# First-half attention units over natural keys in one softmax, and class-ordered copies of the second-half queries

## The chip, the core and the metric

One core of a Trainium2 chip runs the whole kernel. Its engines work side by side, each with its own queue: TensorE (PE in the profile; PEld is its loading of stationary operands), VectorE (DVE), ScalarE (ACT), GpSimd (POOL), and SyncE (SP), which issues nearly all DMAs. The metric is the device time of one execution in microseconds (us). The kernel before took 1133.38 us in the median of three runs (1132.27 to 1135.93).

## The reference

One decoder layer: sequence 1024, width 1024, float32. The input is normalised and projected once; a quarter of the width goes through causal mean pools, three quarters through 12 attention heads of 64; both results share one output projection; then follows a gated feed-forward block. Each head is attended three times, with keys at distances up to 128 (every key), up to 512 (every 4th) and up to 2048 (every 16th), and the three results are merged by their softmax denominators:

```python
DILATED_CONFIGS = ((128, 1), (512, 4), (2048, 16))
for window, dilation in DILATED_CONFIGS:
    o, lse = dilated_branch(q, k, v, window, dilation)   # softmax of s over valid keys; o = e/den @ v
w = softmax(stack(lses), axis=0)
o = sum(w[..., None] * stack(outs), axis=0)
```

Merging by denominators is the same as one softmax over the union of the three key sets in which a key that belongs to two or three of them counts twice or three times.

## The kernel before

All products run on TensorE with float32 data split in a high and a low part: a projection step is three 512-column matmuls. Every matmul is recorded at L276 (`mm`), every transpose at L279 (`turned_to`).

Attention is cut into 12 **units**: six head pairs, each with a first half (queries 0 to 511, `h = 0`) and a second half (queries 512 to 1023, `h = 1`). A unit treats two heads and has four kinds of steps:

- *Scores* (`scores`, L705 on). Each head has a natural side (`side 0`, mask `mA`, the last 128 keys) and a class side (`side 1`, mask `mB`, positions that agree modulo 4). For each of four blocks of 128 queries two matmuls, for the high and the low query part (`qh`, `ql`), write one row block to a PSUM bank with tag `s`, of which there are two. On the class side the stationary operand is `slice(j, 512, 4)`, every fourth query. Where `sg` is 0, `pull()` puts one or more projection matmuls (the *filler*) ahead of each such score matmul. DVE takes the bank with mask and minimum (L750), ACT takes the exponential with its sum (L753).
- *Join* (`merge`, `join`, L758 on). The two sides have their own minima and sums; eleven small DVE instructions, an exponential and two tiny matmuls (`ps_s<-ex,ls`) bring them to common weights `wv`.
- *Weighing* (`weigh`, L801 on). 16 scalings of `pp` by `wv`, most on POOL (L816), some on DVE (L814) or ACT (L812).
- *Values* (`values`, L844 on). `turn` transposes up to four 128 x 128 blocks to a bank `t` (two banks) and splits them to `ptr` (ACT L861, DVE L862); `product` multiplies them by `v`, high and low part. The groups are listed in `GROUPS` (L836).

Keys are stored by class (`k`, position modulo 4 outermost); natural key blocks are read with a strided view. The value rows are in DRAM (`vd`); `v_load` (L672 on) loads a natural (`v0`) and a class-ordered (`v1`) copy for each half.

Order: `put(steps, lo, hi)` places steps on a time axis whose unit is one attention unit, from numbers in `PRM` (L30 to L260); `emit` sorts all steps by these places. A clock with estimated latencies (`await_`) may pull filler steps ahead of a step that would wait. TensorE keeps exactly the written order (`keep_in_program_order`); on the other engines a scheduler places the instructions by priority (`rank`, table `hk`), and each engine then works through its queue in order. Each PE wait in the attention part therefore stops the whole PE stream behind it.

Of the kernel before, what the change touches and what calls it, by code (L numbers as in the profile page):

```python
# [8 lines left out]
F32 = mybir.dt.float32  # L9
# [34 lines left out]
 'n0': 0.12632,
 'n1': 0.36647,
 'h0': {'s0': 0.02145,
        's1': 0.42346,
        'm': 0.62035,
        'w0': 0.78144,
        'w1': 1.2041,  # L50
        't0': 0.85648,
        't1': 1.83344,
        'v0': 1.2506,
        'v1': 2.02168},
 'h1': {'s0': 0.0,
        's1': 0.55,
        'm': 0.63061,
        'w0': 0.77607,
        'w1': 1.33988,
        't0': 0.97415,  # L60
        't1': 1.84958,
        'v0': 1.09414,
        'v1': 1.95434,
        'u0': 0.15852,
        'u1': 0.10633,
        'u2': 0.23141,
        'u3': 0.53154},
# [12 lines left out]
 'pe': 1,  # L80
 'cut': {7: (1, 6, 17)},
# [1846 lines left out]
```

## Time and profile before

| | us |
|---|---|
| median of three runs | 1133.38 |
| the profiled execution's own time | 1133.22 |
| its span in the profile | 1131.4 |
| PE busy | 1115.9 |
| DVE busy | 806.1 |
| ACT busy | 559.9 |
| POOL busy | 549.0 |

Attention runs from about 55 to 400 us of the span, the output projection and the norms until about 490, and the feed-forward block to the end. A matmul's busy time in the profile is longer than its share of the stream, since matmuls overlap; the pitch, from one start to the next, is what the stream pays. Rows of the timeline give the start and the length of a run of like instructions, so the next row's start gives the pitch.

### The profile page before, as it was taken

The page shows a single profiled execution, that of the slowest core. Times are in us where ns is not written, and L with a number is a line of the kernel's source. Part 1 is how long each engine was busy: PE and PEld are TensorE (multiplying, and loading weights), DVE is VectorE, ACT ScalarE, POOL GpSimd, SP SyncE. Part 2 cuts the span into 40 slices and gives each one's busy share as a digit, 9 for nine tenths or more (in the row PEclk, how much of TensorE's full clock was granted, in tenths as well). Part 3 has the DMA queues.
Part 4 walks back from the last instruction along what each step waited for, and adds up shares of the span by engine and source line. Part 5 has one row for each costly group of instructions (what it writes and reads, how often), then busy time and mean ns, then how long its engine had stood idle before and what let it go on. Part 6 is the DMA issues. An engine that isn't in the chain of part 4 may idle for free.

```text
span 1131.4 us, 16902 instructions
## 1 busy us (share of the span) xinstructions
PE 1115.9 (99%) x5922; PEld 958.3 (85%) x5922; DVE 806.1 (71%) x1516; ACT 559.9 (49%) x1068; POOL 549.0 (49%) x481
## 2 busy tenths in 40 slices
PE   9999999999999999999999999999999999999997
PEld 7888999999898888888888888888888888888896
DVE  7967888887998675989777777665676462343684
ACT  8466667666677563966422222332222534343441
POOL 0122646253466222010267767775577896666521
PEclk9999999999999999999999999999999999999999
DMA  8215242415146555672566666434444896556442
GB/s 283 93 70 187 80 146 75 149 57 168 57 130 219 193 191 218 262 280 109 200 235 242 235 233 233 168 143 163 169 168 176 287 348 220 188 195 202 132 149 75
DMA packets 91156, 201.59 MB, mean 178 GB/s; under 512 B 9280, under 2 KB 25152, under 8 KB 89664
## 3 DMA queue, kind: packets, MB, share of 16 engines
q1 hardware_dynamic: 90096, 199.74, 50.5%
q8 instruction: 46, 0.75, 0.3%
q10 hardware_dynamic: 976, 0.79, 0.2%
q14 instruction: 38, 0.31, 0.1%
HBM read 143.61 MB, written 56.89 MB: 177 GB/s over the span
## 4 chain that ended last, share of the span: by engine, by line
PE 90%; DVE 5%; DMA 2%; POOL 1%; ACT 1%; issue 1%; ACTq 0%; SPq 0%; POOLq 0%
PE ps_pj L276 27%; PE ps_s L276 26%; PE ps_o L276 24%; PE ps_t L276 10%; PE ps_t L279 2%; DMA mixd<-mix 1%; POOL pp L816 1%; DVE pp L750 1%; DVE ptr L862 1%; DMA m<-mixd 1%; DVE rsw L512 0%; ACT pp L753 0%; DVE ql L544 0%; DMA wraw<-in_w_in_dram 0%; DVE rco L513 0%
## 5 line engine op out<-in xcount | busy, mean ns | idle before, releaser
L276 PE MATMUL ps_o<-tT,fw 128*128 128x512 f32 x648 | 150.5, 389 | 0.0
L276 PEld LDWEIGHTS ps_o<-tT,fw 128*128 128x128 f32 x648 | 121.5, 188 | 25.4 <-DVE p L1551 0.2
L276 PE MATMUL ps_pj<-x,whl 128*128 128x512 f32 x480 | 138.1, 407 | 0.3 <-DVE whl L324 0.3
L816 POOL TENSOR_SCALAR pp<-pp,wv 128x256 f32<-128x256 f32 (+1 forms) x135 | 67.4, 518 | 111.8 <-DVE wv L796 111.8
L1368 POOL TENSOR_TENSOR fw<-rw,fw 128x512 fp32r<-128x512 f32 x72 | 99.8, 1409 | 31.1 <-ACT fw L1366 31.1
L753 ACT ACTIVATE pp<-pp,sx 128x128 f32<-128x128 f32 (+1 forms) x192 | 89.3, 467 | 32.2 <-DVE sx L750 31.5
L276 PEld LDWEIGHTS ps_pj<-x,whl 128*128 128x128 f32 x480 | 85.0, 189 | 11.1 <-DVE whl L324 0.7
L1663 POOL TENSOR_TENSOR op<-rw,op 128x512 fp32r<-128x512 f32 x38 | 62.2, 1636 | 31.2 <-ACT op L1662 30.6
L350 POOL TENSOR_TENSOR nrr<-nrr,half 128x4 f32<-128x4 f32 (+1 forms) x7 | 7.1, 1013 | 144.3 <-ACT eps L349 102.3
L324 POOL TENSOR_TENSOR whl<-wraw,whl 128x512 fp32r<-128x512 f32 x42 | 54.7, 1323 | 45.7 <-ACT whl L320 43.5
L276 PE MATMUL ps_s<-b,fw 128*128 128x512 f32 x312 | 72.5, 389 | 0.0
L276 PEld LDWEIGHTS ps_s<-b,fw 128*128 128x128 f32 x312 | 58.6, 188 | 12.2
L276 PE MATMUL ps_pj<-whl,x 128*128 128x256 f32 (+1 forms) x432 | 68.4, 300 | 0.0
L1366 ACT ACTIVATE fw<-rw 128x1024 fp32r<-128x1024 f32 x45 | 47.5, 1061 | 41.4 <-PE ps_o L276 16.3
L1368 POOL TENSOR_TENSOR whl<-rw,whl 128x512 fp32r<-128x512 f32 x30 | 47.0, 1587 | 42.4 <-ACT whl L1366 20.8
L1662 ACT ACTIVATE op<-rw 128x1024 fp32r<-128x1024 f32 x38 | 40.0, 1059 | 55.3 <-PE ps_t L276 35.8
L862 DVE TENSOR_TENSOR ptr<-ps_t,ptr 128x512 fp32r<-128x512 f32 (+1 forms) x84 | 55.3, 665 | 11.5 <-ACT ptr L861 10.6
L861 ACT ACTIVATE ptr<-ps_t 128x512 fp32r<-128x512 f32 (+1 forms) x84 | 47.3, 577 | 26.7 <-PE ps_t L279 23.4
L276 PEld LDWEIGHTS ps_pj<-whl,x 128*128 128x128 f32 x432 | 58.2, 191 | 1.7
L1664 DVE TENSOR_TENSOR op<-rw,op 128x512 fp32r<-128x512 f32 x33 | 28.5, 864 | 40.2 <-ACT op L1662 36.1
L276 PE MATMUL ps_s<-k,qh 128*128 128x128 f32 (+1 forms) x192 | 54.3, 294 | 1.9 <-DVE sx L750 1.5
L276 PE MATMUL ps_o<-ptr,v 128*128 128x128 f32 (+1 forms) x472 | 55.5, 255 | 0.2 <-DVE ptr L862 0.2
(328 smaller groups left out, 2856.1 us busy)
## 6 DMA issues: line engine op xcount, KB each, us to landing
rw<-bd SPq DMA_DIRECT2D x77, 256.0 KB, 4.0
rw<-in_w_gate_dram SPq DMA_DIRECT2D x28, 512.0 KB, 4.7
rw<-in_w_up_dram SPq DMA_DIRECT2D x28, 512.0 KB, 5.6
v<-vd SPq DMA_DIRECT2D x22, 512.0 KB, 4.8
rw<-wsd SPq DMA_DIRECT2D x44, 256.0 KB, 3.9
bd<-p SPq DMA_DIRECT2D x39, 256.0 KB, 2.0
rw<-in_w_down_dram SPq DMA_DIRECT2D x33, 256.0 KB, 4.1
wraw<-in_w_out_dram SPq DMA_DIRECT2D x15, 512.0 KB, 4.5
```

Source lines behind the costliest of these rows:

```text
L276: return tc.keep_in_program_order(nc.tensor.matmul(*a, **k))
L279: return tc.keep_in_program_order(nc.tensor.transpose(dst, src, by))
L324: pin(eng.tensor_tensor(dst[:, 1, at:at + w], src[:, at:at + w], dst[:, 0, at:at + w].bitcast(F32), ALU.subtract))
L753: nc.scalar.activation(pt[:, j, lo:], pt[:, j, lo:], AF.Exp, bias=sx[:, 0, side, j, hd, 0:1], scale=-1.0, accum_out=sx[:, 0, side, j, hd, ...
L816: nc.gpsimd.tensor_scalar(pv, pv, un.wv[:, side, j, hd:hd + 1], 1.0, op0=ALU.mult, op1=ALU.mult)
L861: nc.scalar.activation(ptr[:, 0, :w], t[:, :w], AF.Copy)
L862: nc.vector.tensor_tensor(ptr[:, 1, :w], t[:, :w], ptr[:, 0, :w].bitcast(F32), ALU.subtract)
L1366: nc.scalar.activation(dst[:, :, 0], src, AF.Copy)
L1368: low[0] = eng.tensor_tensor(dst[:, i, 1], src[:, i], dst[:, i, 0].bitcast(F32), ALU.subtract)
L1662: nc.scalar.activation(w[:, :, 0], raw, AF.Copy)
L1663: nc.gpsimd.tensor_tensor(w[:, 0, 1], raw[:, 0], w[:, 0, 0].bitcast(F32), ALU.subtract)
L1664: (nc.gpsimd if p == "P1" else nc.vector).tensor_tensor(w[:, 1, 1], raw[:, 1], w[:, 1, 0].bitcast(F32), ALU.subtract)
```

## The change

1. **First-half units** (`dense`, new). The 512 queries see only keys 0 to 511, so each query block of 128 is scored once against all natural keys up to its own (128, 256, 384 or 512 columns). A new mask `mD` (128 x 512, one more load) adds the logarithm of how often a key counts. One softmax gives the weights: no join, no `ex` matmuls; `factor` takes one reciprocal per head. A bank holds one 512-wide row block, or 384 + 128, or 256 + 256. There are 8 scalings instead of 16 (`dense_step`), 10 transposes a head instead of 11, and 4 key blocks of value products, each for all later queries at once, from `v0` alone.
2. **Second-half units** (`q_classes`, new). The queries are copied to class order once per unit (`qc`): the high part by two copies on POOL, the low part by two on ACT (`qe`), 0.3 of a unit ahead of it (`qc: -0.3`). The class-side score matmuls read 128 adjacent queries from `qc`. The `pull()` ahead of each is gone, and `sg` with it. The join is split: its first two DVE instructions (`others`), then an `await_`, then the rest.
3. `v_load` loads `v0` of the first half alone at first, then the other three.
4. Most of the numbers in `PRM` are new: places of steps, priorities, which engine takes a scaling, a split or a rope addition.

Counted over the program, TensorE has 5640 matmuls and transposes written instead of 5856, that is 36 fewer a pair: 16 scores, 2 transposes, 16 value products, 2 `ex`. DVE has 144 mask-and-minimum instructions instead of 192, each with its read, 58 fewer two-operand ones and 15 fewer scalings. POOL has 88 scalings instead of 135, 12 copies and 6 more two-operand instructions.

Three places in the order of instructions. First TensorE in the first half of pair 1 (unit 2). `qh`, `ql_97` are the query parts, `k` the keys, `x_...,whl` is filler for the next pair's projections. Before, at one of its class-side groups:

```order
L276 MATMUL ps_pj<-x_121,whl 128x512
L276 MATMUL ps_s<-k,qh 128x128
L276 MATMUL ps_pj<-x_121,whl 128x512
L276 MATMUL ps_s<-k,ql_97 128x128
L276 MATMUL ps_pj<-x_121,whl 128x512
L276 MATMUL ps_s<-k,qh 128x128
L276 MATMUL ps_pj<-x_122,whl 128x512
L276 MATMUL ps_s<-k,ql_97 128x128
```

Now, the first three of the unit's five score steps:

```order
L287 MATMUL ps_s<-k,qh 128x512
L287 MATMUL ps_s<-k,ql_97 128x512
L287 MATMUL ps_pj<-x_118,whl 128x512 x3
L287 MATMUL ps_s<-k,qh 128x384
L287 MATMUL ps_s<-k,ql_97 128x384
L287 MATMUL ps_s<-k,qh 128x128
L287 MATMUL ps_s<-k,ql_97 128x128
L287 MATMUL ps_pj<-x_119,whl 128x512 x3
L287 MATMUL ps_pj<-x_120,whl 128x512 x3
L287 MATMUL ps_s<-k,qh 128x256
L287 MATMUL ps_s<-k,ql_97 128x256
```

The alternation of narrow scores and single filler matmuls is gone; fewer and wider scores stand in runs, with filler in threes between them.

Second, TensorE at the second half of pair 4 (unit 10), around the values of unit 9 (`ptr`). Before:

```order
L276 MATMUL ps_s<-k,qh 128x256
L276 MATMUL ps_s<-k,ql_97 128x256
L276 MATMUL ps_s<-k,qh 128x256
L276 MATMUL ps_s<-k,ql_97 128x256
L276 MATMUL ps_pj<-whl,x_120 128x256 x3
L276 MATMUL ps_pj<-whl,x_121 128x256 x3
L279 MATMUL ps_t<-pmt,pp 128x128 x4
L276 MATMUL ps_s<-k,qh 128x256
L276 MATMUL ps_s<-k,ql_97 128x256
L276 MATMUL ps_s<-k,qh 128x256
L276 MATMUL ps_s<-k,ql_97 128x256
```

Now:

```order
L290 MATMUL ps_t<-pmt,pp 128x128 x7
L287 MATMUL ps_pj<-whl,x_122 128x256 x3
L287 MATMUL ps_pj<-whl,x_123 128x256 x3
L287 MATMUL ps_s<-k,qh 128x256
L287 MATMUL ps_s<-k,ql_97 128x256
L287 MATMUL ps_s<-k,qh 128x256
L287 MATMUL ps_s<-k,ql_97 128x256
L287 MATMUL ps_s<-k,qc 128x256 x8
L287 MATMUL ps_o<-ptr,v_3837 128x4x4x32
L287 MATMUL ps_o<-ptr,v_3837 64x4x4x32
```

Before, other work stood between two groups of four score matmuls; now three groups, which need three banks of the two, stand in one run (one with `qh` and `ql`, two with `qc`).

Third, POOL around the query copies of pair 1 (`wd` are the new first-half weights, `whl<-wraw` the split of a projection weight). Before, from the scalings of that pair's first half on:

```order
L816 TENSOR_SCALAR pp<-pp,wv 128x128 x3
L816 TENSOR_SCALAR pp<-pp,wv 128x256
L816 TENSOR_SCALAR pp<-pp,wv 128x128 x4
L816 TENSOR_SCALAR pp<-pp,wv 128x256 x3
L324 TENSOR_TENSOR whl<-wraw,whl 128x512 x2
L514 TENSOR_TENSOR rsw<-rsw,sinr 128x512
L517 TENSOR_TENSOR rcl<-rco,rsw 128x128x4
```

Now:

```order
L905 TENSOR_SCALAR pp<-pp,wd 128x384
L905 TENSOR_SCALAR pp<-pp,wd 128x256
L652 COPY qc<-qh 128x512 x2
L335 TENSOR_TENSOR whl<-wraw,whl 128x512 x4
L529 TENSOR_TENSOR rcl<-rco,rsw 128x128x4
```

There are two scalings here where eleven were, the copies stand behind them, and behind the copies stand the weight splits for the filler.

The diff, cut to its core (of the table of numbers a few lines):

```diff
- 'we': (1, 1, 0, 0, 0, 0, 1, 0, 0, 1, 1, 1),
+ 'we': (1, 0, 1, 0, 0, 0, 0, 0, 0, 0, 1, 0),
...
+        'qc': -0.3},
...
- 'sg': (0, 0, 0, 0, 0, 1, 0, 0, 0, 0, 1, 1),
- 'tv': (0, 0, 0, 0, 0, 1, 0, 0, 1, 0, 0, 1),
+ 'tv': (0, 1, 0, 1, 0, 1, 0, 1, 1, 1, 0, 0),
+ 'dw': (0, 0, 0, 2, 1, 0, 0, 0),
...
+ 'qe': ((0, 2), (0, 2), (0, 2), (0, 2), (0, 2), (0, 2))}
...
+    mD = cload(maskD, [P, 512], "mD", qkp)
...
+    def q_classes(pr):
+        pr.qc = []
+        for n in range(2):
+            src = pr.q[1][n]
+            to = qkp.tile([P, 2, 512], F32R, name="qc", tag="qc%d" % n, bufs=1)
+            by, from_ = to.rearrange("p a (c r) -> p a c r", c=4), src.rearrange("p a (r c) -> p a c r", c=4)
+            eng = G["qe"][pr.p][n]
+            for a in range(2):
+                if eng == 2:
+                    nc.scalar.activation(by[:, a], from_[:, a], AF.Copy)
+                else:
+                    (nc.vector if eng else nc.gpsimd).tensor_copy(by[:, a], from_[:, a])
+            pr.qc.append(to)
...
-        return [lambda h=h: load(h) for h in range(2)]
+        return [lambda: load((0, 0)), lambda: load((1, 0), (1, 1), (0, 1))]
...
+    def dense(pr, un):
+        un.sx = small.tile([P, 2, 2, 4], F32, name="sd", tag="sd", bufs=2)
...
+            for hd, j in blocks:
+                w = (j + 1) * P
+                so[hd, j] = s[:, at:at + w]
+                at += w
+                for n in range(2):
+                    mm(so[hd, j], q[n][:, hd, j * P:(j + 1) * P], view(pr.k[:, hd], 0, [[P, 4], [1, 32 * (j + 1)]]),
+                       start=(n == 0), stop=(n == 1))
...
+                    nc.vector.tensor_tensor_reduce(
+                        by_rows, by_class(so[hd, j]), mD[:, 512 - (j + 1) * P:].rearrange("p (r c) -> p r c", c=4),
+                        op0=ALU.add, op1=ALU.min, scale=-0.125, scalar=3e38, accum_out=sx[:, 0, hd, j:j + 1])
+                    nc.scalar.activation(r, r, AF.Exp, bias=sx[:, 0, hd, j:j + 1], scale=-1.0,
+                                         accum_out=sx[:, 1, hd, j:j + 1])
...
+                nc.vector.reciprocal(un.wv[hd], un.sx[:, 1, hd])
...
+        return [lambda: step([(0, 3)]), lambda: step([(0, 2), (0, 0)]), lambda: last(0, (0, 1), (1, 1)),
+                lambda: step([(1, 3)]), lambda: last(1, (1, 2), (1, 0))]
...
-            q, kc = pr.q[h], pr.k
+            q, kc = pr.qc if side else pr.q[h], pr.k
...
-                qs = slice(j * P, (j + 1) * P) if side == 0 else slice(j, 512, 4)
+                qs = slice(j * P, (j + 1) * P)
...
-                    if side and not G["sg"][turn_of(pr, h)]:
-                        pull()
...
-    GROUPS = ([[(1, r, r, 1) for r in range(4)],
-               [(0, 0, 0, 1), (0, 0, 1, 0), (0, 1, 1, 1), (0, 1, 2, 0)],
-               [(0, 2, 2, 1), (0, 2, 3, 0), (0, 3, 3, 1)]],
+    GROUPS = ([[(0, j) for j in range(4)], [(1, j) for j in range(1, 4)], [(2, 2), (2, 3), (3, 3)]],
...
+            if h == 0:
+                for kb in sorted({kb for kb, j in g}):
+                    wd = (4 - kb) * P
+                    oo = view(o[hd], 32 * kb, ([[32, 4 - kb]] if kb < 3 else []) + NAT)
+                    v = pr.v[0, 0][:, kb, hd]
+                    mm(oo, v.rearrange("p a f -> p (a f)"), ptr[:, 0, n * P:n * P + wd],
+                       start=(kb == 0), stop=False, skip_group_check=True)
+                    mm(oo[0:64], v[:, 0], ptr[:, 1, n * P:n * P + wd], start=False, stop=(kb == 3), skip_group_check=True)
+                    n += 4 - kb
...
+        if h:
+            put([lambda pr=pr: q_classes(pr)], u + g["qc"], 0)
+            put([lambda a=(pr, h): merge(*a)], u + g["m"], 0)
```

More of the change, by code (lines that the diff above doesn't have):

```diff
@@ new lines @@
+        'u2': 0.41454,
+        'u3': 0.53154,
+        'qc': -0.3},
+ 'f0': 7e-05,
+ 'f1': -0.00185,
+ 'first': {'s0': 0.526,
+           's1': 0.68454,
+           'm': 0.84275,
+           'w0': 0.75,
+           'w1': 0.96155,
+           't0': 1.1,
+           'v0': 1.3,
+           'v1': 1.94598},
+ 'vt': ((1.09517, 1.10518),
+        (2.83002, 3.26626),
+        (4.77155, 5.38909),
+        (6.76078, 7.29364),
+        (8.75641, 10.31491),
+        (9.91793, 10.41054)),
+ 'pw': (-0.11144, -0.10043, -0.01308),
@@ L758, in merge @@
     def merge(pr, h):
-        with tc.high_priority(offset=rank("j", pr, h)):
-            join(pr, h)
-    def join(pr, h):
         need(("s", pr.p, h), 8)
@@ L766, in join, with others @@
         un = pr.un[h]
+        with tc.high_priority(offset=rank("j", pr, h)):
+            ex = others(un)
+        due["e",] = clock[0] + G["je"]
+        await_(("s", 0), ("e",))
+        with tc.high_priority(offset=rank("j", pr, h)):
+            join(un, ex)
+        for i in range(17):
+            due["w", pr.p, h, i] = clock[0] + G["lw"][0] + G["lw"][1] * i
+    def others(un):
+        ex = small.tile([P, 2, 4, 4, 4], F32, name="ex", tag="ex", bufs=1)
+        own = un.sx[:, 0].rearrange("p s j a b -> p s j (a b)")
+        for sd in range(2):
+            nc.vector.tensor_tensor(ex[:, sd], own[:, 1 - sd][:, None].to_broadcast([P, 4, 4, 4]),
+                                    qd[1 - sd][:, :, None, None].to_broadcast([P, 4, 4, 4]), ALU.mult)
+        return ex
+    def join(un, ex):
         sx = un.sx
-        ex = small.tile([P, 2, 4, 4, 4], F32, name="ex", tag="ex", bufs=1)
-        own = sx[:, 0].rearrange("p s j a b -> p s j (a b)")
         e = bank("s")
@@ L848, in values, with weighted @@
         turned, o = {}, {}
+        def weighted(hd, gi):
+            return "w", pr.p, h, (8 * hd + 8 - 4 * groups[gi][0][0] if h else 4 * hd + 4)
         def turn(hd, gi):
             g = groups[gi]
-            need(("w", pr.p, h, hd, g[0][0]), 4)
-            await_(("t", 0), ("w", pr.p, h, 8 * hd + 8 - 4 * g[0][0]))
+            if h:
+                need(("w", pr.p, h, hd, g[0][0]), 4)
+            else:
+                need(("w", pr.p, 0, hd), 4)
+            await_(("t", 0), weighted(hd, gi))
             t = bank("t")
-            for n, (side, kb, qs, part) in enumerate(g):
+            for n, (kb, j) in enumerate(g if h == 0 else ()):
+                turned_to(t[:, n * P:(n + 1) * P], un.row(hd, j)[:, kb * P:(kb + 1) * P], pmt)
+            for n, (side, kb, qs, part) in enumerate(g if h else ()):
                 turned_to(t[:, n * P:(n + 1) * P], un.pp[hd, side][:, qs, part * P:part * P + P],
@@ L911, in both @@
                 await_(*([("t", 0), ("t", 1)] if new else []),
-                       *(("w", pr.p, h, 8 * hd + 8 - 4 * groups[gi][0][0]) for hd, gi in new),
+                       *(weighted(*a) for a in new),
                        *(("ptr", pr.p, h, *a) for a in old), ("v", pr.p, h))
```

155 lines of the change are left out of this document (96 added, 59 removed), and 320 rows, old and new, of the table PRM.

## The prediction

> **What bounds the kernel now.** I read the page, then the busy time by stage, then PE's waits, then the stream itself.
>
> ```profile
> span 1131.4 us, 16902 instructions
> PE 1115.9 (99%) x5922; PEld 958.3 (85%) x5922; DVE 806.1 (71%) x1516; ACT 559.9 (49%) x1068; POOL 549.0 (49%) x481
> ...
> PE 90%; DVE 5%; DMA 2%; POOL 1%; ACT 1%; issue 1%; ACTq 0%; SPq 0%; POOLq 0%
> ```
>
> PE is busy for all but 15.5 us, and the chain that ended last is 90% PE. By stage (window, its length, then busy PE, PEld, DVE, ACT, POOL, clock, DMA share, GB/s):
>
> ```profile
> 0.00:55.00 55.00, 53.27 (x233) 43.23 (x234) 47.36 (x70) 34.40 (x50) 5.45 (x10) 1.00 0.56 192
> 55.00:400.00 345.00, 337.48 (x2261) 308.42 (x2260) 279.13 (x833) 232.25 (x628) 148.21 (x193) 1.00 0.38 127
> 400.00:900.00 500.00, 500.00 (x2306) 416.15 (x2305) 361.23 (x461) 198.85 (x283) 264.09 (x197) 1.00 0.56 205
> 900.00:1131.40 231.40, 225.20 (x1128) 190.50 (x1126) 118.38 (x154) 94.43 (x109) 131.24 (x82) 0.99 0.58 192
> ```
>
> The change works in the second row. PE idles 345 - 337.5 = 7.5 us there, in waits like these:
>
> ```profile
> PE ps_t L279 <- POOL pp L816: 2.0, 1, 2.0
> PE ps_o L276 <- DVE dhl L999: 1.6, 2, 0.9
> ...
> PE ps_s L276 <- DVE sx L750: 1.5, 3, 0.7
> PE ps_pj L276 <- DMA m<-mixd: 1.2, 1, 1.2
> ```
>
> So attention is bound by the length of the PE stream. Removed PE work shortens the kernel one for one as long as the other engines feed the rest; removed DVE or ACT work shortens nothing by itself, and at most 7.5 us of idle can go.
>
> **Prices of the PE stream.** These timeline rows (start, length, group, count) give the pitches; the next row's start is what counts.
>
> ```profile
> 117.75 0.22 PE L276 MATMUL ps_s<-k,qh 128*128 128x128 f32 x1
> 117.81 0.45 PE L276 MATMUL ps_pj<-x,whl 128*128 128x512 f32 x1
> 118.10 0.22 PE L276 MATMUL ps_s<-k,ql 128*128 128x128 f32 x1
> ...
> 128.60 0.23 PE L276 MATMUL ps_s<-k,qh 128*128 128x128 f32 x1
> ...
> 129.06 0.60 PE L279 MATMUL ps_t<-pmt,pp 128*128 128x128 f32 x4
> 129.42 0.71 PE L276 MATMUL ps_o<-ptr,v 128*128 128x256 f32 x4
> 129.97 0.28 PE L276 MATMUL ps_s<-k,qh 128*128 128x256 f32 x1
> ...
> 130.44 0.64 PE L276 MATMUL ps_pj<-whl,x 128*128 128x256 f32 x4
> ...
> 136.61 0.55 PE L276 MATMUL ps_s<-ex,ls 128*128 128x64 f32 x4
> 136.97 1.92 PE L276 MATMUL ps_pj<-whl,x 128*128 128x256 f32 x14
> ...
> 138.73 0.80 PE L276 MATMUL ps_o<-ptr,v 128*128 128x128 f32 x8
> 139.36 0.62 PE L279 MATMUL ps_t<-pmt,pp 128*128 128x128 f32 x4
> ...
> 206.18 0.48 PE L276 MATMUL ps_s<-k,qh 128*128 128x256 f32 x1
> ...
> 207.20 1.54 PE L276 MATMUL ps_pj<-x,whl 128*128 128x512 f32 x6
> 208.58 0.28 PE L276 MATMUL ps_s<-k,qh 128*128 128x256 f32 x1
> ```
>
> Read from them: a 512-column matmul 1.38 / 6 = 0.23 us; four adjacent 256-column scores 130.44 - 129.97 = 0.47, so 0.12 each; four 256-column scores with every fourth query as stationary operand 207.20 - 206.18 = 1.02, so 0.25 each; a strided 128-column score with a filler 0.35 - 0.23 = 0.12 for the score; two 128- and two 256-column scores 0.46; four transposes 0.36; eight 128-column value products 0.63; four 256-column ones 0.55; the four `ex` records of a join 0.36. By interpolation 384 columns cost 0.175, and 128 in a run about 0.10.
>
> [...]
>
> **The change on PE, part by part.**
> - First-half scores. Before, a unit has 16 strided 128-column scores (16 x 0.12 = 1.9) and four natural groups (2 x 0.46 + 2 x 0.47 = 1.9), 3.8 in all. Now, for two heads and two query parts, 4 x (0.10 + 0.12 + 0.175 + 0.23) = 2.5. Six units: 6 x 1.3 = 7.8 us.
> - Second-half scores. Of the 24 class-side groups in the order of before, 15 stand bare as at 206.18 (units 5, 10, 11 and three where the filler had run out) and win 1.02 - 0.47 = 0.55 each, 8.2 us. In the other nine a 512-column filler already hides the slow load: nothing.
> - First-half values. Before, a head costs 0.63 + 0.55 + about 0.37 (two products of 256, two of 128) = 1.55. Now, high and low, 2 x (0.23 + 0.175 + 0.12) + 0.16 = 1.2. Twelve heads: 4.1 us.
> - Two transposes fewer a pair, 6 x 2 x 0.09 = 1.1 us; six joins fewer, 6 x 0.36 = 2.2 us.
>
> Sum: 7.8 + 8.2 + 4.1 + 1.1 + 2.2 = 23.4 us. As the pitches are read to 0.02 us, the ends are 20 and 26.
>
> **What lies beside PE.** Rows of the attention stretch by shape:
>
> ```profile
> L750 DVE CUSTOM_DVE_ANT_0 pp<-ps_s,mA 128x256 f32<-128x256 f32 x82 | 31.8, 418 | 8.0 <-PE ps_s L276 7.8
> L750 DVE CUSTOM_DVE_ANT_0 pp<-ps_s,mB 128x128 f32<-128x128 f32 x48 | 11.8, 285 | 3.4 <-PE ps_s L276 3.2
> L750 DVE DVE_READ_ACCUMULATOR2_ANT sx<- 128x1 f32 x189 | 15.5, 82 | 0.0
> L773 DVE TENSOR_TENSOR ex<-sx,qdB 128x64 f32<-128x64 f32 x11 | 5.3, 484 | 1.4 <-ACT pp L753 1.4
> L796 DVE TENSOR_TENSOR wv<-total,ps_s 128x16 f32<-128x16 f32 x11 | 1.9, 170 | 0.3
> L816 POOL TENSOR_SCALAR pp<-pp,wv 128x256 f32<-128x256 f32 x84 | 45.4, 557 | 29.8 <-DVE wv L796 29.8
> L514 POOL TENSOR_TENSOR rsw<-rsw,sinr 128x512 f32<-128x512 f32 x12 | 15.5, 1293 | 64.8 <-DVE rsw L512 64.8
> L861 ACT ACTIVATE ptr<-ps_t 128x512 fp32r<-128x512 f32 x61 | 35.6, 592 | 14.8 <-PE ps_t L279 12.6 <-PE ps_o L276 1.7
> ```
>
> - DVE in a first-half unit: 10 x 0.285 + 6 x 0.418 + 16 x 0.08 = 6.6 us becomes 2 x (0.285 + 0.418 + 0.55 + 0.68) + 8 x 0.08 = 4.5 (0.13 per further 128 columns); the join's eleven small instructions, each between 0.17 and 0.48, some 3 us, become two reciprocals. That is 4.7 a unit, 28 us: DVE goes from 279 of 345 (81%) to about 251 of 322 (78%). It wins nothing directly, but says that the shorter PE stream is not fed worse on average.
> - The query copies: 12 on POOL, 12 on ACT, none on PE. POOL has no such row; the bounds are 2 x 0.557 = 1.1 (a scaling, twice as wide) and 1.3 us (L514); I take 1.3, since a strided read will hardly be faster. Twelve are 16 us on an engine that is busy 148 of 345 and loses about half of 96 first-half scalings. ACT's, 12 x 0.6 = 7 us, fit beside the eight exponentials a unit that go. Cover: they are placed 0.3 of a unit (345 / 12 = 29, so 8 us) ahead of the scores that read them. Without that cover the PE stream waits for up to two copies, 2.6 us a unit.
> - While POOL works, DVE can stand still:
>
> ```profile
> 36.98 0.68 DVE L517 TENSOR_TENSOR turned<-turned 128x512 f32<-128x512 f32 x1
> ...
> 238.75 2.53 POOL L324 TENSOR_TENSOR whl<-wraw,whl 128x512 fp32r<-128x512 f32 x2
> ...
> 239.25 2.98 DVE L517 TENSOR_TENSOR rcl<-rco,rsw 128x512 f32<-128x512 f32 x1
> ```
>
>   The DVE addition took 2.98 us and ended 0.9 after POOL's two splits; the like addition at 36.98 took 0.68. [...] So POOL's copies can hold DVE up, by at most 16 us in all, and PE only where DVE is late already.
> - The run of three score groups at unit 10. The third group needs the bank that the second-last one filled, 0.47 us of PE work earlier; DVE needs 2 x (0.42 + 0.08) = 1.0 us for a bank and may be one bank behind. This wait costs 0.5 to 2 us; I take 1.5. Behind it stand the products of unit 9 and the output projection, all on PE.
> - One more load of 256 KB (`mD`) on SP at the start, and value loads in another order. Masks are first read at 58.84 us, far behind their issue; a value load that comes late would cost up to its landing time, 4.8 us, once:
>
> ```profile
> 58.84 0.29 DVE L750 CUSTOM_DVE_ANT_0 pp<-ps_s,mB 128x128 f32<-128x128 f32 x1
> ...
> v<-vd SPq DMA_DIRECT2D x22, 512.0 KB, 4.8
> ```
>
>   I take 0 and keep 0 to 5.
> - New places elsewhere. From 400 to 900 us PE is busy for all 500 us, so nothing can be won there; the splits moved between POOL and DVE (`fe`) are hidden by DVE's idle 139 us, and cost a few us if not.
>
> **The sum.** Against the profiled execution's own 1133.2 us, which is the median within 0.2: 1133.2 - 23.4 + 1.5 = 1111 us, with the 7.5 us of idle unchanged apart from that wait. Its own range is 1107 to 1115.
>
> **Rivals.**
> - *Part of the gain goes into new waits.* Transposes now often come eight at a time on two banks (`tv`), and DVE, at 78%, meets more of them at once. If each of the 12 units waits 0.75 us more, it is 1111 + 9 = 1120. For it speaks that DVE is behind at 239 us; against it, that it has less to do.
> - *The idle goes too.* DVE's 28 us remove the waits on it and the first halves wait for no join: 1133.2 - 23.4 - 6 = 1104. PE's longest waits are on POOL, DVE and DMA alike, so all of them would have to shift well.
> [...]
> - *Slower: the copies come late.* On POOL they stand behind scalings that wait for first-half weights and among splits of 1.3 us. A queue of two splits, three scalings and two copies is about 8 us, just the lead they have. It decides from 23.4 / 6 = 4 us of PE wait per second-half unit on; at 6 us it is 1111 + 36 = 1147. Against it: the queries are projected in the first third of the unit before.
> - *No net change*, 1130 to 1137, if waits of 2 us a unit at the copies or transposes eat the sum.
>
> **Chances.** My forecast 0.60, new waits 0.19, idle goes too 0.10, copies win nothing 0.04, late copies 0.04, no net change 0.03. All but the last two are faster by over 0.3% (3.4 us, about what a measurement here can tell from no change): faster 0.93, same 0.03, slower 0.04. The range is 1104 to 1121: it takes in the forecast, most of the new waits, the worthless copies and the edge of the better case.
>
> **What will show it.** Right: 216 fewer matmuls in attention; class-side scores at 0.12 us in runs; first-half scores at 0.10 to 0.23; PE idle of the attention part still 6 to 11 us, now in a stretch some 22 us shorter; a wait of 1 to 2 us at the three score groups of unit 10; the feed-forward part as long as before. Wrong: PE waits on ACT or POOL at `qc`, waits of `ps_t` on DVE `ptr` in most units, or a stretch after 400 us with PE idle.

## The result and the profile after

The changed kernel took 1121.43 us in the median of six runs (1118.24 to 1123.9), the kernel before 1134.89 beside it: a ratio of 0.9884, 95% interval 0.9863 to 0.9904. It is faster by 1.2%, where 2.0% were forecast; 1121.4 stands just outside the range of 1104 to 1121. The profiled execution took 1118.24 us.

The page of the changed kernel (span, engines, shares of the chain that ended last):

```profile
span 1116.3 us, 16151 instructions
PE 1095.8 (98%) x5694; PEld 929.8 (83%) x5694; DVE 786.2 (70%) x1347; ACT 562.3 (50%) x992; POOL 561.5 (50%) x452
...
PE 85%; DVE 6%; ACT 3%; POOL 2%; DMA 2%; issue 2%; ACTq 0%; SPq 0%; POOLq 0%
```

By stage (columns as in the prediction). To compare like with like, the first two rows end at corresponding matmuls, a `ps_s<-m,whl` near the end of attention behind which equally many matmuls are left: it starts at 399.21 us in the kernel before (first row) and at 384.06 us in the changed kernel (second row). The third row is the changed kernel's stretch behind attention:

```profile
55.00:399.21 344.21, 336.69 (x2258) 307.76 (x2257) 278.34 (x830) 231.57 (x625) 148.21 (x193) 1.00 0.38 127
55.00:384.06 329.06, 316.82 (x2030) 279.65 (x2029) 256.53 (x667) 233.29 (x549) 153.37 (x162) 0.99 0.38 133
380.00:885.00 505.00, 504.97 (x2333) 419.99 (x2331) 366.07 (x467) 203.70 (x296) 270.18 (x198) 1.00 0.56 205
```

From that matmul to the end of the span it takes 732.2 us in both kernels, so all of the gain of these two profiles, 15.1 us, lies ahead of it. There PE idles 329.06 - 316.82 = 12.2 us instead of 7.5, and the clock of that row is 0.99 instead of 1.00. PE's waits there (who waited for whom: total, times, longest):

```profile
PE ps_o L287 <- DMA v<-vd: 2.3, 1, 2.3
PE ps_o L287 <- DVE ptr L973: 2.2, 4, 0.9
PE ps_t L290 <- DVE ptr L973: 1.5, 2, 1.2
PE ps_o L287 <- ACT ptr L972: 1.5, 2, 0.7
...
PE ps_s L287 <- DVE sx L834: 0.5, 1, 0.5
```

The longest is a value load, which before was not in the list; three more rows, 5.2 us, are waits for `ptr`, the split transposes. Nobody waits for `qc`.

**The value load.** The last pair's first natural value rows go to the tile that holds the cosines, and so the load waits for the last reader of that tile (times from the timeline):

```profile
340.90 0.69 DVE L525 TENSOR_TENSOR rco<-ps_pj,cosr 128x512 f32<-128x512 f32 x1
...
341.62 0.36 SPq L718 DMA_DIRECT2D v<-vd  x1
...
350.17 1.06 PE L287 MATMUL ps_o<-ptr,v 128*128 128x512 f32 x4 [2.32 <-DMA v<-vd]
```

The load is issued at 341.62, as soon as that reader ends, and PE goes on at 350.17, 8.5 us later; the median landing of such a load is 4.9 us over the whole run, but 8.8 us for the two that are issued between 330 and 352 us (their median). In this stretch the profile has the DMA engines busy all the time (a share of 1.08 and 409 GB/s in the third row here; windows of 3.41 us, columns as in the stages):

```profile
190.85:194.26 3.41, 2.09 (x18) 1.81 (x19) 2.67 (x5) 3.19 (x5) 1.10 (x2) 1.00 0.03 6
194.26:197.67 3.41, 3.41 (x19) 3.41 (x18) 1.38 (x2) 1.81 (x4) 2.38 (x2) 0.50 0.48 157
...
347.86:351.27 3.41, 1.10 (x6) 0.90 (x7) 3.32 (x11) 2.80 (x9) 2.16 (x2) 1.00 1.08 409
351.27:354.68 3.41, 3.41 (x15) 3.12 (x14) 1.69 (x3) 2.87 (x8) 1.35 (x2) 0.50 1.03 420
```

**Half speed.** The same rows show something that the attention part of before does not have. In 194.26 to 197.67 and in 351.27 to 354.68 the granted clock is 0.50; each time the 3.41 us ahead of it had PE busy for 2.09 or 1.10 us only. In the second of them three 512-column matmuls take 353.64 - 352.22 = 1.42 us, 0.47 each, where such a matmul cost 0.23 in the kernel before:

```profile
352.22 1.63 PE L287 MATMUL ps_pj<-m,whl 128*128 128x512 f32 x3
353.64 0.41 PE L287 MATMUL ps_s<-k,qh 128*128 128x256 f32 x1
```

By estimate from these rows each such period costs half of its length, 1.7 us of PE work, beside the wait itself.

### The profile page after: what moved, and what is told of

Same layout as the page of the kernel before. It is cut to its first block, busy times and chain, and to the rows that moved or that the text cites. A ratio compares the mean times of both kernels' runs of the same rounds, so it can differ in the third digit from the quotient of the medians.

```text
span 1116.3 us, 16151 instructions
## 1 busy us (share of the span) xinstructions
PE 1095.8 (98%) x5694; PEld 929.8 (83%) x5694; DVE 786.2 (70%) x1347; ACT 562.3 (50%) x992; POOL 561.5 (50%) x452
## 4 chain that ended last, share of the span: by engine, by line
PE 85%; DVE 6%; ACT 3%; POOL 2%; DMA 2%; issue 2%; ACTq 0%; SPq 0%; POOLq 0%
PE ps_s L287 25%; PE ps_pj L287 24%; PE ps_o L287 24%; PE ps_t L287 10%; PE ps_t L290 2%; DVE ql L556 1%; DVE ptr L973 1%; DMA v<-vd 1%; POOL whl L335 1%; DVE qh L555 1%; ACT pp L773 1%; DVE pp L770 1%; POOL pp L921 1%; DMA vd<-vs 1%; DVE rsw L524 1%
## 5 line engine op out<-in xcount | busy, mean ns | idle before, releaser
L1490 POOL TENSOR_TENSOR fw<-rw,fw 128x512 fp32r<-128x512 f32 x74 | 103.3, 1421 | 66.5 <-ACT fw L1488 66.5
L287 PE MATMUL ps_pj<-x,whl 128*128 128x512 f32 x480 | 127.6, 399 | 0.9 <-DVE vs L685 0.6
L335 POOL TENSOR_TENSOR whl<-wraw,whl 128x512 fp32r<-128x512 f32 x46 | 61.8, 1365 | 61.3 <-ACT whl L331 51.4
L1490 POOL TENSOR_TENSOR whl<-rw,whl 128x512 fp32r<-128x512 f32 x32 | 51.2, 1621 | 47.6 <-DMA rw<-in_w_up_dram 29.8
L287 PE MATMUL ps_pj<-whl,x 128*128 128x256 f32 (+1 forms) x432 | 65.3, 301 | 0.8 <-POOL whl L335 0.8
L287 PE MATMUL ps_o<-ptr,v 128*128 128x128 f32 (+3 forms) x376 | 50.4, 268 | 6.2 <-DMA v<-vd 2.3
L921 POOL TENSOR_SCALAR pp<-pp,wv 128x256 f32<-128x256 f32 x57 | 30.5, 556 | 49.2 <-DVE wv L890 49.2
L1785 POOL TENSOR_TENSOR fw<-rw,fw 128x512 fp32r<-128x512 f32 x26 | 42.6, 1640 | 21.5 <-ACT fw L1784 18.1
L837 ACT ACTIVATE pp<-pp,sx 128x256 f32<-128x256 f32 x96 | 47.9, 501 | 9.3 <-DVE sx L834 8.9
```

The lines of the kernel that those rows point to most:

```text
L287: return tc.keep_in_program_order(nc.tensor.matmul(*a, **k))
L335: pin(eng.tensor_tensor(dst[:, 1, at:at + w], src[:, at:at + w], dst[:, 0, at:at + w].bitcast(F32), ALU.subtract))
L837: nc.scalar.activation(pt[:, j, lo:], pt[:, j, lo:], AF.Exp, bias=sx[:, 0, side, j, hd, 0:1], scale=-1.0, accum_out=sx[:, 0, side, j, hd, ...
L921: nc.gpsimd.tensor_scalar(pv, pv, un.wv[:, side, j, hd:hd + 1], 1.0, op0=ALU.mult, op1=ALU.mult)
L1490: low[0] = eng.tensor_tensor(dst[:, i, 1], src[:, i], dst[:, i, 0].bitcast(F32), ALU.subtract)
L1785: nc.gpsimd.tensor_tensor(w[:, 0, 1], raw[:, 0], w[:, 0, 0].bitcast(F32), ALU.subtract)
```

## The experiments

Each kernel ran beside the kernel before on the same chip. The expectations were written against medians; the comparisons here go by the ratio to before, since before itself read 1134.9 us beside the changed kernel and 1133.3 to 1133.7 beside the experiments. At 1133.6 us for before the changed kernel's ratio is 1120.5 us. Times "by ratio" below are made so. The intervals are 1 to 2.5 us wide to each side, so a difference of two of these times is known to 2 to 3 us.

| kernel | median us | ratio to before, 95% | by ratio us |
|---|---|---|---|
| changed | 1121.43 | 0.9884 (0.9863 to 0.9904) | 1120.5 |
| before + copies (b_qc) | 1131.34 | 0.9987 (0.9978 to 0.9995) | 1132.1 |
| no copies, slow loads (a_noqc) | 1120.33 | 0.9883 (0.9870 to 0.9896) | 1120.3 |
| no copies, fast loads (a_nocopy) | 1110.73 | 0.9806 (0.9790 to 0.9823) | 1111.6 |
| copies unread, slow loads (a_copyunused) | 1125.46 | 0.9922 (0.9907 to 0.9937) | 1124.8 |
| POOL's copies alone, fast loads (a_hi) | 1119.19 | 0.9878 (0.9864 to 0.9892) | 1119.8 |
| ACT's copies alone, fast loads (a_lo) | 1115.07 | 0.9837 (0.9819 to 0.9855) | 1115.1 |
| low part on DVE (a_qe_dve) | 1127.18 | 0.9941 (0.9928 to 0.9953) | 1126.9 |
| all on POOL (a_qe_pool) | 1118.12 | 0.9868 (0.9847 to 0.9889) | 1118.6 |
| all on ACT (a_qe_act) | 1121.63 | 0.9897 (0.9882 to 0.9912) | 1121.9 |
| high on ACT, low on POOL (a_20) | 1117.08 | 0.9852 (0.9839 to 0.9866) | 1116.8 |
| value rows elsewhere (a_vroom) | 1116.73 | 0.9851 (0.9838 to 0.9863) | 1116.7 |
| the last two together (av_20) | 1115.43 | 0.9834 (0.9821 to 0.9848) | 1114.8 |
| all on POOL + value rows (a_qe_pool_v) | 1118.01 | 0.9863 (0.9843 to 0.9883) | 1118.1 |
| no copies, filler, value rows (a_noqc_pull_v) | 1118.43 | 0.9871 (0.9856 to 0.9885) | 1119.0 |
| groups one at a time (a_tv0b) | 1127.12 | 0.9942 (0.9930 to 0.9955) | 1127.0 |

### First four: the copies, their engine, the value load

**b_qc**, the kernel before with `q_classes` and its `put` (at u - 0.3):

```diff
-            q, kc = pr.q[h], pr.k
+            q, kc = pr.qc if side and h else pr.q[h], pr.k
-                qs = slice(j * P, (j + 1) * P) if side == 0 else slice(j, 512, 4)
+                qs = slice(j * P, (j + 1) * P) if side == 0 or h else slice(j, 512, 4)
```

> The kernel before, with the query copies of the second halves alone (high part on POOL, low part on ACT, 0.3 of a unit ahead); fillers, joins and first halves stay as they were. Theory, the prices of the PE stream: the 15 groups of four class-side scores that stood bare win 0.55 us each, 1134.9 - 8.2 = 1126.7. Rival 1, the copies cost on ACT and POOL what they win on PE: 1131 to 1135. Rival 2, the slow load has nothing to do with the stride: 1135 or more, and the class-side scores stay at 0.25 us.

Measured 0.9987, a gain of 0.05% to 0.22%. The copies won a small part of the 8.2 us. In the profile the matmul that stood at 399.21 us starts at 397.01:

```profile
55.00:397.01 342.01, 332.73 (x2258) 301.16 (x2257) 283.67 (x831) 243.89 (x637) 165.27 (x205) 1.00 0.38 128
```

That is 2.2 us earlier, although PE idles 9.3 us instead of 7.5 and one period of half speed, at 354.4 us, costs 1.7 us by the estimate above. So the stream itself became some 5.7 us shorter, an estimate, and new waits and the half speed took more than half of it.

**a_noqc**, the changed kernel without the copies:

```diff
-            q, kc = pr.qc if side else pr.q[h], pr.k
+            q, kc = pr.q[h], pr.k
-                qs = slice(j * P, (j + 1) * P)
+                qs = slice(j * P, (j + 1) * P) if side == 0 else slice(j, 512, 4)
-            put([lambda pr=pr: q_classes(pr)], u + g["qc"], 0)
```

> The changed kernel without the query copies: the class-side scores of all second halves read every fourth query again, with no filler between them. Theory: 24 groups lose 0.55 us each, 13.2 us, and the waits that the copies cause around 191 and 249 us (2.7 us and a half-speed period of 1.7) go: 1121.4 + 13.2 - 4.4 = 1130. Rival 1, the copies cost nothing: 1134.6. Rival 2, they cost what they win: 1121 or less.

Measured 0.9883, no different from the changed kernel with all its copies. So the change without its copies, that is the first halves and the new places, makes the whole gain, and the copies cost about what they win. (How much of it is the first halves and how much the places was not separated.)

**a_vroom**, the value rows in a tile that is free earlier:

```diff
+            if (nat, h) == (1, 0) and pr.p == 4:
+                return att.tile([P, 4, 2, 2, 64], F32R, name="v1", tag="cosr", bufs=1)
+            if (nat, h) == (0, 0) and pr.p == 5:
+                return att.tile([P, 4, 2, 2, 64], F32R, name="v0", tag="v10", bufs=1)
-        (9.91793, 10.41054)),
+        (9.5, 10.41054)),
```

> The changed kernel with the natural value rows of the last pair's first half in the tile v10, which is free two units earlier, and its load placed at 9.5 instead of 9.92; the class-ordered rows of pair 4, which are read later, take its old place. Theory: the 2.3 us wait at 347.9 us goes and with it the half-speed period that begins at 351.3 (1.7 us): 1121.4 - 4.0 = 1117.4. Rival 1, the half-speed period is not tied to this wait: 1119.1. Rival 2, the stream waits there for something else that is as late (splits, another load): 1121.

Measured 0.9851: 3.8 us by ratio, as the first theory has it (the interval doesn't exclude the 2.3 of rival 1). The wait is gone, and PE keeps its clock in the stretch where it had fallen to half; this profile has another period of half speed instead, at 251.3 us, which that of the changed kernel does not have:

```profile
347.48:350.90 3.42, 3.11 (x21) 2.79 (x22) 3.33 (x14) 3.37 (x11) 1.65 (x3) 1.00 1.05 395
350.90:354.30 3.40, 3.34 (x18) 2.54 (x17) 3.34 (x12) 3.40 (x10) 1.99 (x2) 1.00 1.06 420
```

**a_qe_dve**, the low part on DVE:

```diff
- 'qe': ((0, 2), (0, 2), (0, 2), (0, 2), (0, 2), (0, 2))}
+ 'qe': ((0, 1), (0, 1), (0, 1), (0, 1), (0, 1), (0, 1))}
```

> The changed kernel with the low part of the query copies on DVE instead of ACT. Theory: the ACT copies of 1.14 us delay the splits that follow them, so the PE waits around 191 and 249 us (2.7 us) and the half-speed period at 194.3 (1.7 us) go: 1121.4 - 4.4 = 1117. Rival, DVE is the busier engine (254 of 325 us in the attention stretch, ACT 230), and what ACT wins DVE loses, its own splits coming later: 1121 to 1126.

Measured 0.9941, at the far end of the rival. One place of its timeline shows why (second half of pair 1):

```profile
136.47 2.85 POOL L652 CAST qc<-qh 128x512 fp32r<-128x512 f32 x2
...
136.82 3.04 DVE L556 TENSOR_TENSOR ql<-rco,qh 64x512 fp32r<-64x512 f32 x2
...
139.89 3.17 DVE L652 CAST qc<-ql 128x512 fp32r<-128x512 f32 x2
142.99 1.27 DVE L973 TENSOR_TENSOR ptr<-ps_t,ptr 128x512 fp32r<-128x512 f32 x2
143.72 0.96 PE L290 MATMUL ps_t<-pmt,pp 128*128 128x128 f32 x4 [4.19 <-DVE ptr L973]
```

Beside POOL's copies `ql` takes 3.04 us for two; the DVE copies stand behind it, `ptr` behind them, and PE waits 4.19 us.

### Two more engines, filler, and the groups

**a_qe_pool** and **a_qe_act** set `qe` to (0, 0) and (2, 2) in all pairs.

> The changed kernel with all four copies of a unit on POOL. Theory A, what costs is the two ACT copies of 1.14 us that stand ahead of splits in ACT's queue: they go, 1121.4 - 4 = 1117. Theory B, what costs is POOL's copies, beside which DVE's instructions take two to four times as long (qh 1.64 instead of 0.43 at 186.8 us): twice as many, 1126. If both cost alike: 1121.

> The changed kernel with all four copies of a unit on ACT, none on POOL. Theory A, ACT's queue: 4.6 us of copies ahead of splits instead of 2.3, 1126 or more. Theory B, POOL's copies beside DVE: qh and ql on DVE take their 0.43 and 0.71 us again, 1117. If both cost alike: 1121.

Measured 0.9868 and 0.9897: 1.9 us better and 1.4 us worse by ratio, each within the intervals. Neither theory alone holds. (The slow `qh` that the first expectation names is no sign of the copies: its 1.64 us at 186.81 are those of two instructions, and in a_nocopy the two take 1.64 us as well, at 186.72, beside POOL's scalings; in the mean one of DVE's takes 0.52 in the changed kernel and 0.53 in a_nocopy. What the copies lengthen is `ql`, 0.92 instead of 0.71 us in the mean.)

**a_noqc_pull_v** is a_noqc with a_vroom and, ahead of the class-side score matmul,

```diff
+                    if side and turn_of(pr, h) in (1, 3, 7):
+                        pull()
```

> The changed kernel without query copies, with a filler step ahead of each class-side score matmul in units 1, 3 and 7 as in the kernel before, and with the last pair's value rows in v10. Theory: the filler hides the slow load of strided queries in some 9 of 24 groups, 9 x 0.55 = 5 us, and the value rows give 4.7 as they did alone: 1120.3 - 5 - 4.7 = 1110.6. Rival, the copies' absence leaves nothing to win, or filler that is used up here is missing later: 1116.

Measured 0.9871, a miss: 1.3 us better than a_noqc by ratio, where 9.7 were expected. The value rows did not give their 3.8 us here, or the filler lost them again; which was not settled.

**a_tv0b** does the groups singly where `tv` is 1:

```diff
-            put([lambda i=i, f=part: f(2, i) for i in range(ng // 2 + 1)], u + lo, u + lo + (hi - lo) * (ng + 2) / ng)
+            d = (hi - lo) / ng
+            put([lambda i=i, f=part: f(0, i) for i in range(ng)], u + lo, u + hi)
+            put([lambda i=i, f=part: f(1, i) for i in range(ng)], u + lo + 1.5 * d, u + hi + 1.5 * d)
```

> The changed kernel with transposes and products in turn, one group at a time, in the six units in which they come two groups at a time; the stretch that they fill is the same. Theory of the rival in the prediction (pairs of groups on two banks wait for DVE): the 3 us of PE waits on ptr around 191, 249 and 306 us go with one half-speed period, 1121.4 - 4.7 = 1117. Rival, the waits on ptr come from what stands ahead of the splits in ACT's and DVE's queues: 1121 or more.

Measured 0.9942, 6.5 us slower by ratio. So transposing two groups at a time, on which the prediction's rival of new waits rested, helps where it was put, and nothing is won by undoing it. With the groups apart PE waits more for `ptr` and for the value load:

```profile
PE ps_o L287 <- DVE ptr L973: 10.4, 8, 1.9
PE ps_o L287 <- DMA v<-vd: 4.9, 1, 4.9
```

### The copies' work and the fast loads, apart

In these two, a_noqc and the changed kernel TensorE has the same instructions in the same order; only the stride of the class-side loads and the copies differ.

**a_nocopy** has neither copies nor strides:

```diff
-            q, kc = pr.qc if side else pr.q[h], pr.k
+            q, kc = pr.q[h], pr.k
-            put([lambda pr=pr: q_classes(pr)], u + g["qc"], 0)
```

> The changed kernel without the copies, but with the fast loads: the class-side score matmuls of the second halves read 128 adjacent queries of the uncopied tiles (so those scores belong to other queries); TensorE's order is that of the changed kernel. Theory A, the copies' own work on POOL and ACT costs what the loads win: it takes 24 x 0.4 to 0.55 us off the kernel without copies, 1120.3 - 10 to 13 = 1107 to 1110. Theory B, a faster stream only runs into waits that the slow loads had covered: 1118 to 1121.

**a_copyunused** makes the copies and reads the strided tiles (the first two edits of a_noqc).

> The changed kernel with all copies made but read by nobody: the class-side scores read every fourth query of the old tiles. TensorE's order is that of the changed kernel. Theory A, the copies' own work costs 8 to 11 us: 1120.3 + 8 to 11 = 1128 to 1131. Theory B, the copies are hidden: 1120 to 1122.

| by ratio, us | slow loads | fast loads | fast loads win |
|---|---|---|---|
| no copies | 1120.3 | 1111.6 | 8.7 |
| copies made | 1124.8 | 1120.5 | 4.3 |
| copies cost | 4.5 | 8.9 | |

Theory A holds for the fast loads; where the loads are slow the copies cost about half of what was expected (the two costs, 8.9 and 4.5, differ by little more than their noise). In the timeline of a_noqc a strided weight load takes 0.30 to 0.33 us and a load of adjacent queries 0.19 (one of each; class side, then natural side):

```profile
340.63 0.33 PEld L287 LDWEIGHTS ps_s<-k,ql 128*128 128x128 f32 x1
...
343.02 0.19 PEld L287 LDWEIGHTS ps_s<-k,qh 128*128 128x128 f32 x1
```

In a_nocopy all of these loads take 0.19 (means of 188 and 189 ns for `qh` and `ql`). (In a_noqc the mean of the group `ps_s<-k,ql`, 236 against 189 ns, hides this: only a third of its 144 loads are strided.)

A bare strided group of four, from the timeline of a_noqc, costs 341.46 - 340.53 = 0.93 us, or 0.82 where a 512-column matmul stands ahead (339.00 to 339.82):

```profile
339.00 0.28 PE L287 MATMUL ps_s<-k,qh 128*128 128x256 f32 x1
...
339.82 0.87 PE L287 MATMUL ps_pj<-whl,x 128*128 128x256 f32 x6
340.53 0.40 PE L287 MATMUL ps_s<-k,qh 128*128 128x256 f32 x1
...
341.46 0.76 PE L287 MATMUL ps_pj<-whl,x 128*128 128x256 f32 x5
```

Against 0.48 with the copies (339.88 to 340.36 in the changed kernel) the excess is 0.34 to 0.45 a group and 8 to 11 us for 24, as the loads win in the table without copies.

One place at which the copies cost shows in the timeline of the changed kernel, second half of pair 2:

```profile
188.48 2.38 DVE L556 TENSOR_TENSOR ql<-rco,qh 64x512 fp32r<-64x512 f32 x2
188.74 3.08 POOL L652 CAST qc<-qh 128x512 fp32r<-128x512 f32 x2
189.36 1.15 ACT L650 ACTIVATE qc<-ql 128x512 fp32r<-128x512 f32 x1 [0.65 <-DVE ql L556]
190.53 0.60 ACT L972 ACTIVATE ptr<-ps_t 128x512 fp32r<-128x512 f32 x1
...
191.02 1.11 ACT L650 ACTIVATE qc<-ql 128x512 fp32r<-128x512 f32 x1
191.18 0.33 PE L287 MATMUL ps_o<-ptr,v 128*128 128x128 f32 x1 [0.72 <-ACT ptr L972]
...
192.03 0.58 ACT L972 ACTIVATE ptr<-ps_t 128x512 fp32r<-128x512 f32 x1
192.36 0.90 PE L287 MATMUL ps_o<-ptr,v 128*64 128x128 f32 x8 [0.85 <-DVE ptr L973]
```

and in a_nocopy:

```profile
188.40 1.57 DVE L556 TENSOR_TENSOR ql<-rco,qh 64x512 fp32r<-64x512 f32 x2
188.65 1.09 ACT L972 ACTIVATE ptr<-ps_t 128x512 fp32r<-128x512 f32 x2
...
190.24 0.22 PE L287 MATMUL ps_o<-ptr,v 128*128 128x128 f32 x1
...
191.46 1.48 PE L287 MATMUL ps_o<-ptr,v 128*64 128x128 f32 x15 [1.00 <-DVE ptr L973]
```

With the copies the first split on ACT begins at 190.53 instead of 188.65: ACT's queue has a copy ahead of it, the copy waits for `ql`, and `ql` takes 2.38 instead of 1.57 us because POOL copies beside it. PE waits 0.72 and 0.85 us. Without the copies it waits here too, but 1.00 us and in one place; the transposes behind start at 192.78 instead of 194.02 us. With the copies PE is busy for 2.09 of the 3.41 us from 190.85 to 194.26, shown above, and half speed follows. In the a_nocopy profile no period at half speed lies in attention (a clock of 1.00 in its row below).

### Which copies

**a_hi** and **a_lo** leave one part out (the part that is not copied reads adjacent, other queries):

```diff
         for n in range(2):
+            if n != 0:      # a_lo: n != 1
+                pr.qc.append(pr.q[1][n])
+                continue
```

> The changed kernel with only POOL's copies (high part); the low part of the class-side scores reads 128 adjacent queries of the uncopied tile (so it belongs to other queries). The ends are 1110.7 without any copy and 1121.4 with all. If POOL's copies cost by holding DVE up (ql 0.92 instead of 0.71 us in the mean): most of the 10.7, 1118 or more. If ACT's copies cost by standing ahead of splits: 1111 to 1114. If both cost for themselves and add: 1116.

> The changed kernel with only ACT's copies (low part); the high part reads 128 adjacent queries of the uncopied tile (so it belongs to other queries). If ACT's copies cost by standing ahead of splits: most of the 10.7, 1118 or more. If POOL's cost: 1111 to 1114. If both add: 1116. That moving ACT's copies to POOL won 3.3 us and moving POOL's to ACT nothing speaks for some of both.

By ratio POOL's copies alone cost 8.2 us and ACT's alone 3.5; together 8.9. POOL's are the dearer ones. The four profiles say where the cost lies. TensorE's order is the same in all, so the matmul that stands at 384.06 us in the changed kernel can be looked up in each (a_nocopy's row as an example):

```profile
55.00:375.34 320.34, 313.29 (x2035) 277.59 (x2035) 253.62 (x670) 222.67 (x540) 136.59 (x150) 1.00 0.39 137
```

| kernel | that matmul at, us | PE idle from 55 us to it | of it for `ptr` | for value loads | half-speed periods until it |
|---|---|---|---|---|---|
| no copies (a_nocopy) | 375.34 | 7.1 | 2.2 | 1.6 | 0 |
| ACT's alone (a_lo) | 379.40 | 9.3 | 3.5 | 1.6 | 1 |
| POOL's alone (a_hi) | 383.42 | 12.3 | 4.9 | 3.7 | 2 |
| all (changed) | 384.06 | 12.2 | 5.2 | 2.3 | 2 |

With all copies the matmul comes 8.7 us later than with none: 5.2 us of more idle and two periods at half speed, 3.4 us by the estimate above, make 8.6. For a_lo it is 4.1 against 2.3 + 1.7, for a_hi 8.1 against 5.2 + 3.4. So the copies cost by longer waits for splits and value loads, and by the half speed behind them.

**a_20** swaps the engines (`qe` (2, 0)), so that POOL's copies wait for `ql`; **av_20** adds a_vroom.

> The changed kernel with the engines of the copies swapped: high part on ACT, low part on POOL. POOL's copies now wait for ql, so they can no longer run beside DVE's ql. Theory, the collision of POOL's copies with ql (0.92 instead of 0.71 us in the mean) is what costs: ql takes 0.71 again, and of the 8.5 us that POOL's copies cost alone a good part goes, 1114 to 1117. Rival, POOL's copies slow whatever DVE does then, and ACT's stand ahead of splits as before: 1121.

> The same swap, with the last pair's value rows in v10 as well, against 1116.7 for those rows alone. Theory: 1116.7 - 4 to 7 = 1110 to 1113. Rival, no gain from the swap: 1117.

The swap gave 3.7 us by ratio and `ql` its time back. Changed kernel first (mean ns after the busy time), then a_20:

```profile
L556 DVE TENSOR_TENSOR ql<-rco,qh 64x512 fp32r<-64x512 f32 x20 | 18.4, 920 | 0.4
L652 POOL CAST qc<-qh 128x512 fp32r<-128x512 f32 x12 | 16.8, 1432 | 25.6 <-DVE qh L555 22.2 <-ACT qh L554 3.4
L650 ACT ACTIVATE qc<-ql 128x512 fp32r<-128x512 f32 x12 | 13.5, 1136 | 6.6 <-DVE ql L556 6.6
```

```profile
L652 POOL CAST qc<-ql 128x512 fp32r<-128x512 f32 x12 | 15.4, 1303 | 35.3 <-DVE ql L556 35.3
L556 DVE TENSOR_TENSOR ql<-rco,qh 64x512 fp32r<-64x512 f32 x20 | 14.5, 726 | 0.5
```

The swap also moved ACT's copies, which no longer wait for `ql` and stand right behind `qh`, so the 3.7 us belong to both, and `ql`'s share of them stays open; a_20 is still 5 us above a_nocopy. Joined with the value rows the swap gave 1115.4 us in the median, the fastest here of the kernels that leave nothing out, but only 2 us less by ratio than the value rows alone. a_qe_pool_v, all copies on POOL with the value rows, gave 0.9863 where both gains together would have been 1113.4 us:

> The changed kernel with all copies on POOL and the last pair's value rows in v10: the two edits that helped alone, 3.3 and 4.7 us. If they add: 1121.4 - 8 = 1113.4. If POOL's later splits (a wait of 2.2 us for whl at 332 us in the run with the copies on POOL) take their place: 1116.

These two gains do not add: in its profile PE waits 4.3 us for POOL's weight splits (`whl`). That profile is of the slowest of its four executions, 1122.0 us.

## Why the prediction was wrong

**The PE stream: right in sum.** 23.4 us of stream were forecast to go and 1111 us to be left. With the copies' own work taken away the kernel took 1110.7 (1111.6 by ratio); a value wait of 1.6 us that was not in the sum and a bank wait that is 1 us shorter than forecast nearly cancel in it. In its profile the matmul of 399.21 us starts at 375.34, 23.9 us earlier; 0.5 of that is less idle, so some 23 us of stream went. First-half scores cost what was said: in the changed kernel a 512-column pair takes 61.98 - 61.53 = 0.45, a 384 and 128 group 58.94 - 58.41 = 0.53 us, which with 0.48 for four of 256 columns makes 2.4 a unit against 2.5:

```profile
58.41 0.34 PE L287 MATMUL ps_s<-k,qh 128*128 128x384 f32 x1
...
58.94 0.91 PE L287 MATMUL ps_t<-w,x 128*128 128x512 f32 x3
...
61.53 0.39 PE L287 MATMUL ps_s<-k,qh 128*128 128x512 f32 x1
...
61.98 0.84 PE L287 MATMUL ps_pj<-whl,x 128*128 128x512 f32 x3
```

**Second-half loads: cause right, size off.** 0.55 us a bare group was read from one place; the groups in a_noqc lose 0.34 to 0.45. For the 15 groups that would be 5 to 7 us instead of 8.2, and b_qc's stream lost 5.7. That the sum of 23.4 came out all the same is in part luck: other parts must have given some 2 us more than they were priced at; which ones is open. That the stride makes the load slow here is shown by a_noqc against a_nocopy, 8.7 us with nothing else changed on TensorE, and by the loads themselves: 0.30 to 0.33 us strided against 0.19 adjacent, for the same 128 columns.

**The step that failed: "the query copies", taken at nothing behind a cover of 8 us.** The cover was there, no matmul waited for `qc`. But the cost of a copy is not its lateness to its reader; it is what stands behind it in its engine's queue, and what runs beside it on another engine. The prediction named the second ("POOL's copies can hold DVE up, by at most 16 us in all, and PE only where DVE is late already") and priced it at nothing; alone it was 8.2 us. It did not look at ACT's queue around the splits at all, and ACT's price of 0.6 us a copy, taken from a row that reads without a stride, was 1.14. Together they took 8.9 us of a miss that is 9.5 by ratio, as longer waits of PE for the splits and a value load and as half speed behind them. Half speed was in no term of the sum; two periods of it, 3.4 us by the estimate, are in the changed kernel's attention part. That POOL's copies cost by holding DVE up is shown for `ql` (2.38 instead of 1.57 us for two at 188.48, 0.92 instead of 0.73 in the mean); that all of their 8.2 us come about so is not shown. That the copies cost more where the loads are fast (8.9 against 4.5) fits a stream that leaves the splits less time; this is argued, not shown.

**Value loads, 0 taken and 0 to 5 kept:** the wait was 2.3 us, and moving it away won 3.8 with the half-speed period that followed it. The end of the range was right, the value taken wrong; the landing time stood for the median load, and this one was issued late, by its tile, into a stretch where such loads took 8.8 us. These 3.8 us and the 8.9 of the copies overlap and must not be added: without the copies the same load is waited for 1.6 us instead of 2.3, and no half speed follows.

**The bank wait at unit 10:** 1.5 us taken, 0.5 found (the wait for `sx`). **The idle time, "unchanged apart from that wait":** 12.2 instead of 7.5; without the copies it is 7.1. **After 400 us:** unchanged, as said.

**The rivals.** New waits (1120) came out by size, but not by the mechanism that was given for it: a_tv0b was slower with one group at a time, and in a_nocopy, with the same transposes in the same order, the waits for `ptr` are 2.2 us instead of 5.2. That the copies win nothing (1111 and the 8.2 us of the second-half scores, 1119) came out in sum: the fast loads won 8.7 us (a_noqc against a_nocopy), and the copies' work cost 8.9 (a_nocopy against the changed kernel).

## What to carry to other kernels

Price work that is moved to a half-idle engine by what it delays, not by whether its own result is in time: look in that engine's queue for the instruction on which the bounding engine waits next, and at which instructions of a neighbour run beside it. A kernel that does the new work and reads none of it, and one that reads the fast way without doing it, split gain and cost cleanly where the change as a whole shows almost nothing. And before a load is moved, look at who last reads the tile that it fills.

## What the runs showed of the hardware

A wait cost twice here: the 2.3 us for the value load and, by the estimate above, 1.7 us at half speed behind it. In the attention part of the changed kernel the granted clock was 0.50 for 3.41 us from 194.26 and from 351.27 us on, each time behind 3.41 us in which PE had been busy for 2.09 and 1.10 only. The two periods begin 157.0 us or 46 times 3.413 apart. In a_tv0b PE was idle for a whole stretch of that length, and the two behind it, 6.8 us, were at 0.50:

```profile
355.03:358.44 3.41, 0.00 (x0) 0.00 (x0) 3.23 (x10) 3.36 (x10) 0.13 (x1) 1.00 1.04 392
358.44:361.85 3.41, 2.38 (x10) 2.11 (x10) 0.30 (x1) 1.26 (x3) 0.43 (x1) 0.50 1.06 419
361.85:365.27 3.42, 3.42 (x13) 2.94 (x12) 1.21 (x5) 3.02 (x7) 3.42 (x4) 0.50 1.03 414
```

In a_vroom 3.41 us with 2.25 of them busy were followed by half speed:

```profile
247.90:251.31 3.41, 2.25 (x22) 1.91 (x22) 2.25 (x6) 3.38 (x9) 1.80 (x3) 1.00 0.00 0
251.31:254.72 3.41, 3.41 (x19) 3.41 (x18) 1.85 (x3) 2.35 (x5) 2.52 (x2) 0.50 0.80 248
```

and in the kernel before 3.42 us with 2.09 busy, as much as in the changed kernel's window at 190.85, were followed by full speed:

```profile
348.87:352.29 3.42, 2.09 (x18) 1.88 (x16) 3.32 (x9) 2.10 (x5) 2.93 (x3) 1.00 0.95 297
352.29:355.70 3.41, 2.73 (x17) 2.37 (x18) 3.29 (x8) 2.06 (x4) 3.26 (x7) 1.00 0.79 272
```

So PE's busy time in the stretch ahead, as the profile counts it, does not decide alone; what does is not shown. The changed kernel's six runs granted 0.992 to 0.996 of the clock in the mean.
